# Moving the early channels' final-norm weights from VectorE to GpSimd in the last stage of a hybrid decoder layer

## The chip, the cores and the metric

One core of a Trainium2 chip runs the whole layer in one launch. The metric is the device time of an execution in microseconds (us), as the median of several runs. TensorE does the matmuls, VectorE and ScalarE the elementwise work, GpSimd small things and some DMA issues, SyncE issues most DMAs. In the profile they are PE (matmul), PEld (weight load), DVE (VectorE), ACT (ScalarE), POOL (GpSimd) and SP (SyncE).

## The reference

Tokens: 1024. Channels: 1024. All float32. The layer is a norm, an input projection, a pooling mixer and a recurrent mixer, an output projection, an MLP of width 4096, a gated per-layer input, and a final norm. Only the end bears on this case:

```python
z = rms_norm(h, norm_ple_g[l])
gate = jax.nn.sigmoid(z @ w_ple_gate[l] + b_ple_gate[l])
h = h + gate * (p[l] @ w_ple_proj[l])
return rms_norm(h, norm_final_g)      # h * rsqrt(mean(h*h) + 1e-6) * norm_final_g
```

## The kernel before

Every float32 product is made of three passes over split operands (high by high, high by low, low by high). All through the kernel the channels lie on the partitions and the tokens along the row, with one exception: the last stage. There, for the late 512 tokens and the later 512 channels (the "late" channels, numbers 512 to 1023), the gate product is turned around, so that 128 tokens lie on the partitions. There are four such token tiles, 0 to 3 (`NTOK`), and for each of them a row tile `late[i]` of 128 x 1024: its first half, `quarter(i, 0)`, holds the early channels (0 to 511), which were computed with channels on partitions and have come in turned through DRAM; the second half, `quarter(i, 1)`, holds the late channels.

For a token tile, in this order:

- TensorE: 24 matmuls of 128x512 for the gate into `ps_e` (`gate_products`, L1239) and 6 for the projection of the layer's input into `ps_j` (`token_proj`, L1263; in some tiles it goes to a bank named `ps_e`). The first of the 24 is issued ahead, in the middle of the tile before (`gate_opened`). After it, VectorE adds the gate's bias to what lies in the bank (L1248), and only then may the other 23 accumulate onto it.
- ScalarE: the sigmoid (L1278). VectorE: its product with the projection (L1283), the sum into `quarter(i, 1)` (L1285), and the sum of squares of the late channels (`mean`, L1217), which starts from `early_mean[i]`, the sum of squares of the early channels plus epsilon.
- GpSimd: `inverse(i)`, the power -0.5 of the mean (L1288), 128x1.
- VectorE: `scale_late(i)` (L1292), the late channels times the inverse and the final norm's weights. ScalarE: `scale_early(i)` (L1296), the early channels times the inverse. SyncE: `leave_for(i)` (L1301), the store of both halves.

So the early channels' share of the final norm's weights has to be multiplied in at another place: `early_gain` (L1227), after ScalarE has squared them (`early_square`, L1223), since the squares are those of the channels without weights. Behind it L1228 adds epsilon to their sum.

In this stage every VectorE, ScalarE and TensorE instruction is pinned to the order in which the code issues it (`pin`). So the order of the lines in the loop over `NTOK` is the order in each engine's queue, and an instruction that waits holds up all that stand behind it on its engine. `early(0)` issues the early work of tiles 0 and 1 in iteration 1, `early(2)` that of tiles 2 and 3 at the end of iteration 1.

Of the kernel before, what the change touches and what calls it, by code (L numbers as in the profile page):

```python
# [12 lines left out]
ALU = mybir.AluOpType  # L13
# [6 lines left out]
EPS = 1e-6  # L20
# [20 lines left out]
NTOK = 4  # L41
NQUAD = 4 * P
# [21 lines left out]
def block_kernel(  # L64
# [17 lines left out]
    nc = tc.nc  # L82
# [49 lines left out]
    def bank(name):  # L132
        return pd.tile([P, HALF], F32, tag="pd", name=name)
# [27 lines left out]
    def got(ps):  # L161
        if ps.shape[-1] > HALF:
            return ps.rearrange("p (b j a) -> p b a j", b=2, a=2)
        return ps.rearrange("p (j a) -> p a j", a=2)

    def by(x, ps):
        if ps.shape[-1] > HALF:
            return x.rearrange("p (b a j) -> p b a j", b=2, a=2)
        return x.rearrange("p (a j) -> p a j", a=2)
# [7 lines left out]
    def pin(ins):  # L177
        return tc.keep_in_program_order(ins) if in_order else ins
# [324 lines left out]
    for k in range(NT):  # L503
# [3 lines left out]
        for hs in halves:  # L507
            if k == hs.start == 0:
                whi, wlo = (t[:, :HALF] for t in weight_tiles("wl0"))
                g = col("g_mix", 0)  # L510
                x, zhi, zlo = (t[:, hs] for t in (H[0], *A[0]))
# [9 lines left out]
            x, zhi, zlo = (t[:, hs] for t in (H[k], *A[k]))  # L521
# [597 lines left out]
    early_mean, means, inverses = ([ms[:, 4 * x + i : 4 * x + i + 1] for i in range(NTOK)] for x in range(3))  # L1119
    power = pool.tile([P, 1], F32, name="power")  # L1120
# [60 lines left out]
    g_row, b_row, square = row[:, :S], row[:, S : S + NQUAD], row[:, S + NQUAD :]  # L1181
# [19 lines left out]
    def quarter(i, half):  # L1201
        return late[i][:, half * NQUAD : (half + 1) * NQUAD]
# [9 lines left out]
    def mean(i, cut=slice(0, NQUAD)):  # L1212

        n = cut.stop - cut.start
        x = quarter(i, 1).rearrange("p (g x) -> p g x", g=4)[:, :, cut.start // 4 : cut.stop // 4]
        pin(
            nc.vector.tensor_tensor_reduce(  # L1217
                square[:, :n].rearrange("p (g x) -> p g x", g=4), x, x, 1.0 / D, early_mean[i], ALU.mult, ALU.add, means[i]
            )
        )  # L1220

    def early_square(i):
        pin(nc.scalar.activation(T[5][:, SECOND], quarter(i, 0), AF.Square, scale=D**-0.5, accum_out=early_mean[i]))  # L1223

    def early_gain(i):
        x = quarter(i, 0)
        pin(nc.vector.tensor_tensor(x, x, g_row[:, :NQUAD], ALU.mult))  # L1227
        pin(nc.vector.tensor_scalar_add(early_mean[i], early_mean[i], EPS))  # L1228

    def token_slice(i):  # L1230
        return slice(HALF + i * P, HALF + (i + 1) * P)
# [19 lines left out]
    def token_gate(i, pg):  # L1251
        gate_products(i, pg, range(1, 12))
        ahead = gate_opened(i + 1) if i < NTOK - 1 else None
        gate_products(i, pg, range(12, 3 * NT))
        return ahead

    def token_proj(i, pj, cut):
        ts = token_slice(i)
        for k, (hi, lo, wh, wl) in enumerate(ple):
            for n, (z, w) in enumerate(((hi, wh), (hi, wl), (lo, wh))):  # L1260
                w = w[:, NQUAD + cut.start : NQUAD + cut.stop]
                pin(
                    nc.tensor.matmul(  # L1263
                        pj, z[:, ts], turns(w), start=k == n == 0, stop=k == len(ple) - 1 and n == 2
                    )
                )
# [7 lines left out]
    def sigmoids(i, pg, cut=slice(0, NQUAD)):  # L1274
        t = T[3 + i % 2][:, FIRST]
        whole = cut.stop - cut.start == NQUAD
        got_a, by_a = (got(pg), by(t, pg)) if whole else (got(pg)[:, cut.start // 256], t[:, cut])
        pin(nc.scalar.activation(by_a, got_a, AF.Sigmoid))  # L1278

    def gated(i, pj, cut=slice(0, NQUAD)):  # L1280

        t, e = T[3 + i % 2][:, FIRST][:, cut], T[3 + i % 2][:, SECOND][:, cut]
        pin(nc.vector.tensor_tensor(by(e, pj), by(t, pj), got(pj), ALU.mult))  # L1283
        y = quarter(i, 1).rearrange("p (g o x) -> p g o x", g=4, x=32)[:, :, cut.start // P : cut.stop // P]
        pin(nc.vector.tensor_tensor(y, y, e.rearrange("p (o g x) -> p g o x", g=4, x=32), ALU.add))  # L1285

    def inverse(i):
        nc.gpsimd.tensor_tensor(inverses[i], means[i], power, ALU.pow)  # L1288

    def scale_late(i, cut=slice(0, NQUAD)):  # L1290
        y = quarter(i, 1)[:, cut]
        pin(nc.vector.scalar_tensor_tensor(y, y, inverses[i], g_row[:, NQUAD:][:, cut], ALU.mult, ALU.mult))  # L1292

    def scale_early(i, cut=slice(0, NQUAD)):
        x = quarter(i, 0)[:, cut]
        pin(nc.scalar.activation(x, x, AF.Identity, scale=inverses[i]))  # L1296

    def leave_for(i, cut=slice(0, NQUAD)):
        to = token_out[:, i].rearrange("p (h x) -> p h x", h=2)
        tc.keep_in_program_order(  # L1300
            nc.sync.dma_start(to[:, :, cut], late[i].rearrange("p (h x) -> p h x", h=2)[:, :, cut])  # L1301
        )

    def token_last(i, pg, pj):

        cuts = slice(0, 256), slice(256, NQUAD)
        for cut in cuts:
            sigmoids(i, pg, cut)
        scale_early(i - 1)
        leave_for(i - 1)  # L1310
        gated(i, pj[0], cuts[0])
        y = quarter(i, 1).rearrange("p (g x) -> p g x", g=4)[:, :, :64]
        pin(
            nc.scalar.activation(
                T[5][:, HALF : HALF + 256].rearrange("p (g x) -> p g x", g=4), y, AF.Square, scale=D**-0.5, accum_out=means[i - 1]
            )
        )
        gated(i, pj[1], cuts[1])
        pin(nc.vector.tensor_tensor(early_mean[i], early_mean[i], means[i - 1], ALU.add))
        mean(i, cuts[1])  # L1320
        inverse(i)
        scale_early(i, slice(0, 256))
        rest = quarter(i, 0)[:, 256:]
        pin(nc.vector.tensor_scalar_mul(rest, rest, inverses[i]))
        scale_late(i)
        for half in range(2):
            nc.sync.dma_start(token_out[:, i, half * NQUAD : (half + 1) * NQUAD], quarter(i, half))

    for g, hs in enumerate(GROUPS):
# [3 lines left out]
        for n, o in enumerate(ORDER[g]):  # L1333
# [14 lines left out]
            if g == 0 and 1 <= n < 5:  # L1348
                raw = wp.tile([P, S], F32, tag="raw", name=f"wg0_{n + 3}_raw")
                nc.sync.dma_start(raw, w_gate[n + 3])  # L1350
                x = slice((n - 1) * P, n * P)
# [27 lines left out]
    def early(first):  # L1379

        for x in range(first, first + 2):
            early_square(x)
            early_gain(x)

    in_order[:] = [True]
    opened = gate_opened(0)
    for i in range(NTOK):
        end = i == NTOK - 1
        pg, pj = opened
        if end:  # L1390
            token_gate(i, pg)
            pj = [x[:, :256] for x in (pj, bank("ps_j_end"))]
            for a, x in enumerate(pj):
                token_proj(i, x, slice(256 * a, 256 * a + 256))
            token_last(i, pg, pj)
            continue
        token_proj(i, pj, slice(0, NQUAD))
        opened = token_gate(i, pg)
        if i == 1:
            early(0)  # L1400
            mean(0)
            inverse(0)
        sigmoids(i, pg)
        if i > 0:
            scale_late(i - 1)
            scale_early(i - 1)
            leave_for(i - 1)
        gated(i, pj)
        if i == 0:
            continue  # L1410
        mean(i)
        inverse(i)
        if i == 1:
            early(2)
        if i == 2:
            scale_late(i)
    in_order.clear()
# [82 lines left out]
```

## Time and profile before

| what | value |
|---|---|
| median of 3 runs | 919.86 us (919.85 to 919.89) |
| the profiled execution's own time | 919.68 us |
| its span, first to last instruction | 917.9 us |
| granted TensorE clock | 0.998 |
| TensorE matmul busy, share of the span | 99% |
| VectorE busy | 76% |
| GpSimd busy | 4%, 62 instructions |
| last stage, from the first turned gate matmul | 882.6 us to 917.9 us |

The profiled execution's time is 1.78 us over its span, and it lies 0.18 us below the median of the runs. A row of the timeline reads: start in us, duration in us, engine, line, operation, tile written and tiles read, partitions x columns, how many. In square brackets stands how long the engine had been idle before it and what ended that idle time. The rows of the waits read: who waited, for whom, us in total, times, the longest.

### The profile page before, as it was taken

Reading aid. Unit: us, or ns where it says so; the run is one execution under the profiler, and the core shown is the slowest. Engines: PE = TensorE matmul, PEld = TensorE weight load, DVE = VectorE, ACT = ScalarE, POOL = GpSimd, SP = SyncE. Lnnn points to the kernel's source line nnn. Section 1 sums busy time; section 2 is a strip of 40 time slices with the busy share of each in tenths; the row PEclk is TensorE's granted clock in tenths of the full one; section 3 lists DMA queues with packets and bytes.
Section 4 is the critical chain, followed back from the end, with each engine's and each line's share of the span. In section 5 each row is a group of like instructions: output and inputs, shape, how many; then the busy total and the mean of one; then the engine's idle time right before and its main releaser. Section 6 shows DMA issues by size and latency. Waiting matters only on the chain.

```text
span 917.9 us, 11247 instructions
## 1 busy us (share of the span) xinstructions
PE 907.8 (99%) x4221; PEld 791.2 (86%) x4221; DVE 700.8 (76%) x872; ACT 466.3 (51%) x602; POOL 39.1 (4%) x62
## 2 busy tenths in 40 slices
PE   9999999999999999999999999999999999999996
PEld 7888888888888888888888888888888888888885
DVE  7999974668876567656756899899876679799665
ACT  6569892447554454445444654353343436555322
POOL 4300001000000000000000000000000000000001
PEclk9999999999999999999999999999999999999999
DMA  7211145214478667766864987466633341041363
GB/s 273 101 47 45 48 160 144 76 46 120 111 206 223 201 167 229 224 184 176 243 196 165 355 321 278 138 202 203 205 113 100 115 161 46 1 138 47 104 181 117
DMA packets 56871, 142.47 MB, mean 155 GB/s; under 512 B 4976, under 2 KB 9968, under 8 KB 56816
## 3 DMA queue, kind: packets, MB, share of 16 engines
q1 hardware_dynamic: 52992, 132.31, 43.5%
q0 software_dynamic: 2736, 8.91, 5.8%
q10 hardware_dynamic: 1088, 0.52, 0.3%
q8 instruction: 33, 0.54, 0.3%
q14 instruction: 22, 0.18, 0.1%
HBM read 106.08 MB, written 35.65 MB: 154 GB/s over the span
## 4 chain that ended last, share of the span: by engine, by line
PE 96%; DMA 1%; DVE 1%; issue 1%; SPq 0%; POOL 0%; ACT 0%; DVEq 0%; POOLq 0%; ACTq 0%
PE ps_P_d L363 32%; PE ps_b_u L363 12%; PE ps_i L363 9%; PE ps_o L363 9%; PE ps_d_u L363 8%; PE ps_a_u L363 8%; PE ps_e L363 8%; PE ps_l L363 3%; PE ps_P_u L363 3%; PE ps_l L557 1%; PE ps_j L363 1%; PE ps_g L626 1%; PE ps_l_second L363 1%; PE ps_p L363 1%; DMA turn<-late 0%
## 5 line engine op out<-in xcount | busy, mean ns | idle before, releaser
L363 PE MATMUL ps_P_d<-a,wd_P_hi 128*128 128x512 f32 x880 | 261.8, 379 | 0.0
L363 PEld LDWEIGHTS ps_P_d<-a,wd_P_hi 128*128 128x128 f32 x880 | 166.5, 189 | 23.5
L363 PE MATMUL ps_P_d<-a,wd_P_lo 128*128 128x512 f32 x440 | 166.9, 379 | 0.0
L363 PE MATMUL ps_b_u<-a,wu_P 128*128 128x512 f32 x504 | 113.6, 379 | 0.0
L363 PEld LDWEIGHTS ps_b_u<-a,wu_P 128*128 128x128 f32 x504 | 95.3, 189 | 13.4
L363 PEld LDWEIGHTS ps_P_d<-a,wd_P_lo 128*128 128x128 f32 x440 | 83.2, 189 | 11.7
L363 PE MATMUL ps_a_u<-y,wu_P 128*128 128x512 f32 x360 | 82.6, 379 | 0.0
L363 PEld LDWEIGHTS ps_a_u<-y,wu_P 128*128 128x128 f32 x360 | 68.1, 189 | 9.6
L807 DVE TENSOR_TENSOR t_h<-t_h,ps_P_d 128x512 f32<-128x512 f32 (+1 forms) x56 | 42.4, 758 | 37.0 <-PE ps_P_d L363 37.0
L186 DVE TENSOR_TENSOR a<-wd,a 128x1024 fp32r<-128x1024 f32 x56 | 67.0, 1218 | 0.9 <-ACT a L185 0.6
L363 PE MATMUL ps_i<-a,wi_hi 128*128 128x512 f32 x256 | 66.1, 381 | 0.0
L363 PE MATMUL ps_o<-y,wo_hi 128*128 128x512 f32 x256 | 65.7, 379 | 0.0
L185 ACT ACTIVATE a<-wd 128x1024 fp32r<-128x1024 f32 x56 | 57.9, 1049 | 7.0 <-PE ps_P_d L363 7.0
L363 PEld LDWEIGHTS ps_i<-a,wi_hi 128*128 128x128 f32 x256 | 48.1, 189 | 7.9 <-PE ps_g L626 0.3
L185 ACT ACTIVATE wd_P_hi<-wd 128x1024 fp32r<-128x1024 f32 x24 | 25.3, 1056 | 58.0 <-PE ps_P_d L363 57.9
L363 PEld LDWEIGHTS ps_o<-y,wo_hi 128*128 128x128 f32 x256 | 48.4, 189 | 6.8
L825 DVE SCALAR_TENSOR_TENSOR t_h<-t_h,rstd 128x2048 f32<-128x2048 f32 x16 | 36.6, 2291 | 19.3 <-ACT t_h L844 19.3
L186 DVE TENSOR_TENSOR wu_P<-wu_raw,wu_P 128x512 fp32r<-128x512 f32 x45 | 30.9, 687 | 24.1 <-ACT wu_P L185 23.9
L186 DVE TENSOR_TENSOR wu_P<-wu,wu_P 128x512 fp32r<-128x512 f32 x47 | 32.3, 687 | 21.7 <-ACT wu_P L185 21.6
L363 PE MATMUL ps_d_u<-y,wu_P 128*128 128x512 f32 x180 | 41.3, 379 | 0.0
L363 PE MATMUL ps_d_u<-a,wu_P 128*128 128x512 f32 x180 | 41.3, 379 | 0.0
L185 ACT ACTIVATE wu_P<-wu 128x512 fp32r<-128x512 f32 x47 | 29.4, 625 | 20.0 <-PE ps_b_u L363 14.0
(252 smaller groups left out, 1538.6 us busy)
## 6 DMA issues: line engine op xcount, KB each, us to landing
wd<-act SPq DMA_DIRECT2D x56, 512.0 KB, 5.4
act<-t_h SPq DMA_DIRECT2D x32, 512.0 KB, 6.1
wu<-in_w_up SPq DMA_DIRECT2D x16, 512.0 KB, 4.9
act<-wu SPq DMA_DIRECT2D x16, 512.0 KB, 6.0
wd<-in_w_down SPq DMA_DIRECT2D x16, 512.0 KB, 5.9
wu_raw<-in_w_up SPq DMA_DIRECT2D x15, 512.0 KB, 5.3
t_h<-in_xT SPq DMA_DIRECT2D x14, 512.0 KB, 4.6
wg_raw<-in_w_gate SPq DMA_DIRECT2D x10, 512.0 KB, 3.3
```

The source lines that it names most:

```text
L185: first = pin(nc.scalar.activation(hi, src, AF.Copy))
L186: lowest[:] = [pin((eng or nc.vector).tensor_tensor(lo, src, f32(hi), ALU.subtract)).ins]
L363: ins = nc.tensor.matmul(ps, w, turns(z[:, hs]), start=first and z is zhi and w is whi, stop=last and w is wlo, skip_group_check=more,)
L557: nc.tensor.matmul(ps, kblk(w, o), turns(z[:, hs]), start=k == n == 0, stop=False)
L626: nc.tensor.matmul(x, w[r, o * P : (o + 1) * P], turns(z[r, at : at + HALF]), start=n == 0, stop=n == 2)
L807: (eng or nc.vector).tensor_tensor(to, to if y is None else y, x, ALU.add)
L825: nc.vector.scalar_tensor_tensor(cc, cc, 0.0, twice(R), ALU.max, ALU.mult)
```

## The change

Two things. The product with the weights (L1227, four times, 128x512 each) goes from VectorE to GpSimd, and its place in GpSimd's queue is fixed between the powers: tile 0's ahead of the first power, tile 1's behind it, those of tiles 2 and 3 behind the second. The addition of epsilon (128x1) stays on VectorE, in the place where the product and the addition were. The power is now pinned too.

```diff
     def early_gain(i):
         x = quarter(i, 0)
-        pin(nc.vector.tensor_tensor(x, x, g_row[:, :NQUAD], ALU.mult))
-        pin(nc.vector.tensor_scalar_add(early_mean[i], early_mean[i], EPS))
+        pin(nc.gpsimd.tensor_tensor(x, x, g_row[:, :NQUAD], ALU.mult))
...
     def inverse(i):
-        nc.gpsimd.tensor_tensor(inverses[i], means[i], power, ALU.pow)
+        pin(nc.gpsimd.tensor_tensor(inverses[i], means[i], power, ALU.pow))
...
         for x in range(first, first + 2):
             early_square(x)
-            early_gain(x)
+            pin(nc.vector.tensor_scalar_add(early_mean[x], early_mean[x], EPS))
...
         if i == 1:
             early(0)
+            early_gain(0)
             mean(0)
             inverse(0)
+            early_gain(1)
         sigmoids(i, pg)
...
         if i == 1:
             early(2)
+            for x in range(2, NTOK):
+                early_gain(x)
         if i == 2:
             scale_late(i)
```

In the rows below `late_6384` to `late_6387` are the row tiles of token tiles 0 to 3, `edge` holds the means and inverses, `t_h` the weights' row and scratch, and ISA is the sum of squares (two rows: the work, and the read of its sum). Lines behind L1228 are one less in the changed kernel.

VectorE's queue before, from the sum of squares of tile 1 to the product of tile 2's sigmoid:

```order
L1217 ISA t_h,edge<-late_6385,edge 128x512
L1217 ISA edge 128x1
L1227 TENSOR_TENSOR late_6386<-late_6386,t_h 128x512
L1228 TENSOR_SCALAR edge<-edge 128x1
L1227 TENSOR_TENSOR late_6387<-late_6387,t_h 128x512
L1228 TENSOR_SCALAR edge<-edge 128x1
L1248 TENSOR_TENSOR ps_e_3_6709<-ps_e_3_6709,t_h 128x2x256
L1292 SCALAR_TENSOR_TENSOR late_6385<-late_6385,edge,t_h 128x512
L1283 TENSOR_TENSOR t_h<-t_h,ps_j_2_6655 128x512
```

The same stretch of VectorE's queue in the changed kernel:

```order
L1217 ISA t_h,edge<-late_6385,edge 128x512
L1217 ISA edge 128x1
L1382 TENSOR_SCALAR edge<-edge 128x1 x2
L1247 TENSOR_TENSOR ps_e_3_6709<-ps_e_3_6709,t_h 128x2x256
L1291 SCALAR_TENSOR_TENSOR late_6385<-late_6385,edge,t_h 128x512
L1282 TENSOR_TENSOR t_h<-t_h,ps_j_2_6655 128x512
```

The two products no longer stand ahead of the addition of tile 3's bias (L1248, now L1247). The two of tiles 0 and 1 are likewise gone from ahead of tile 0's sum of squares.

GpSimd's queue in the changed kernel, behind the last DMA that it issues (before there were only the four powers, L1288):

```order
L1227 TENSOR_TENSOR late_6384<-late_6384,t_h 128x512
L1287 TENSOR_TENSOR edge<-edge,power 128x1
L1227 TENSOR_TENSOR late_6385<-late_6385,t_h 128x512
L1287 TENSOR_TENSOR edge<-edge,power 128x1
L1227 TENSOR_TENSOR late_6386<-late_6386,t_h 128x512
L1227 TENSOR_TENSOR late_6387<-late_6387,t_h 128x512
L1287 TENSOR_TENSOR edge<-edge,power 128x1 x2
```

Each of the powers of tiles 0, 1 and 2 now stands behind a product that ends before it can begin.

## The prediction

> **What bounds the kernel now.** I read the page's busy line first, then the waits of TensorE from 880 us on, then the timeline of that stretch, engine by engine.
>
> ```profile
> PE 907.8 (99%) x4221; PEld 791.2 (86%) x4221; DVE 700.8 (76%) x872; ACT 466.3 (51%) x602; POOL 39.1 (4%) x62
> ...
> L363 PE MATMUL ps_P_d<-a,wd_P_hi 128*128 128x512 f32 x880 | 261.8, 379 | 0.0
> ```
>
> TensorE sets the pace nearly everywhere, so the change can win only what TensorE idles in the last stage, or what lies behind its last matmul. In the last stage it waits once:
>
> ```profile
> PE ps_e L1239 <- DVE ps_e L1248: 1.1, 1, 1.1
> ```
>
> and TensorE's part of the timeline shows where:
>
> ```profile
> 897.10 5.34 PE L1239 MATMUL ps_e<-a 128*128 128x512 f32 x24
> 903.51 5.23 PE L1239 MATMUL ps_e<-a 128*128 128x512 f32 x23 [1.06 <-DVE ps_e L1248]
> 908.57 0.83 PE L1263 MATMUL ps_j<-proj,proj 128*128 128x256 f32 x6
> ```
>
> The wait is for the addition of tile 3's bias. One matmul of this size shows 0.38 us (the page's 379 ns), so 24 of them in 5.34 us start every (5.34 - 0.38) / 23 = 0.216 us, and the 25th could have started at 897.10 + 24 x 0.2157 = 902.28. It started at 903.51: 1.23 us late, more than the 1.06 of idle time shown, since matmuls overlap. The 23 after the stall took 5.23, where 22 x 0.2157 + 0.38 makes 5.13: the restart costs 0.10 more. **TensorE's loss is 1.33 us**, and that is the cap on this part. VectorE shows why the bias is late:
>
> ```profile
> 896.53 0.69 DVE L1227 TENSOR_TENSOR late<-late,t_h 128x512 f32<-128x512 f32 x1 [0.81 <-ACT t_h L1223]
> 897.14 0.15 DVE L1228 TENSOR_SCALAR edge<-edge 128x1 f32<-128x1 f32 x1
> 897.20 0.74 DVE L1217 CUSTOM_DVE_ANT_0 t_h<-late,edge 128x512 f32<-128x512 f32 x1
> ...
> 898.64 0.75 DVE L1292 SCALAR_TENSOR_TENSOR late<-late,edge,t_h 128x512 f32<-128x512 f32 x1 [0.69 <-POOL edge L1288]
> 899.31 0.68 DVE L1283 TENSOR_TENSOR t_h<-t_h,ps_e 128x512 f32<-128x512 f32 x1
> 900.03 0.69 DVE L1285 TENSOR_TENSOR late<-late,t_h 128x512 f32<-128x512 f32 x1
> 900.75 0.75 DVE L1217 CUSTOM_DVE_ANT_0 t_h<-late,edge 128x512 f32<-128x512 f32 x1
> ...
> 901.43 0.69 DVE L1227 TENSOR_TENSOR late<-late,t_h 128x512 f32<-128x512 f32 x1
> 902.03 0.15 DVE L1228 TENSOR_SCALAR edge<-edge 128x1 f32<-128x1 f32 x1
> 902.10 0.68 DVE L1227 TENSOR_TENSOR late<-late,t_h 128x512 f32<-128x512 f32 x1
> 902.70 0.15 DVE L1228 TENSOR_SCALAR edge<-edge 128x1 f32<-128x1 f32 x1
> 902.76 0.69 DVE L1248 TENSOR_TENSOR ps_e<-ps_e,t_h 128x512 f32<-128x512 f32 x1
> 903.36 0.74 DVE L1292 SCALAR_TENSOR_TENSOR late<-late,edge,t_h 128x512 f32<-128x512 f32 x1
> 904.02 0.68 DVE L1283 TENSOR_TENSOR t_h<-t_h,ps_j 128x512 f32<-128x512 f32 x1
> 904.73 0.69 DVE L1285 TENSOR_TENSOR late<-late,t_h 128x512 f32<-128x512 f32 x1
> 905.46 0.75 DVE L1217 CUSTOM_DVE_ANT_0 t_h<-late,edge 128x512 f32<-128x512 f32 x1
> ...
> 906.88 0.75 DVE L1292 SCALAR_TENSOR_TENSOR late<-late,edge,t_h 128x512 f32<-128x512 f32 x1 [0.66 <-POOL edge L1288]
> 909.51 0.42 DVE L1283 TENSOR_TENSOR t_h<-t_h,ps_j 128x256 f32<-128x256 f32 x1 [1.88 <-ACT t_h L1278]
> ```
>
> From 896.53 to 903.36 VectorE is a chain whose only rest is 0.69 us for the first power, and three of the products (L1227) stand in it. TensorE resumes 903.51 - 902.76 = 0.75 us after the bias row starts, so a bias that starts by 902.28 - 0.75 = **901.53 costs TensorE nothing**.
>
> **The change, part by part.**
>
> *VectorE loses four products.* Tile 0's (894.96) fell into idle time. For tile 1, VectorE still waits for ScalarE's square, since the addition of epsilon needs its sum; but then 0.06 us later (897.14 to 897.20) comes tile 0's sum of squares, at 896.53 + 0.06 = 896.59 in place of 897.20: 0.61 us earlier. Power, scaling, product, sum and sum of squares of tile 1 move by as much, the last to 900.14. Of the pair at 901.43 and 902.10 the additions stay, at 0.07 each, and 0.60 goes for each product: 1.20 us. The bias starts at 902.76 - 0.61 - 1.20 = **900.95**, which is 0.58 us ahead of what TensorE needs. ScalarE follows: its squares of tiles 2 and 3 stand behind a scaling that waits for the same first power, so they move by the same 0.61.
>
> ```profile
> 894.74 0.19 ACT L1223 ACTIVATION_READ_ACCUMULATOR t_h<-late 128x1 f32 x1
> ...
> 900.54 0.19 ACT L1223 ACTIVATION_READ_ACCUMULATOR t_h<-late 128x1 f32 x1
> 902.48 0.60 ACT L1278 ACTIVATE t_h<-ps_e 128x512 f32<-128x512 f32 x1 [1.75 <-PE ps_e L1239]
> ```
>
> The last sum is then there at 900.73 - 0.61 = 900.12, ahead of the additions at 900.82. The edit costs nothing there.
>
> *GpSimd gets four products.* No row of it has this shape, so its price d has to be bounded. It does run small ones:
>
> ```profile
> 0.72 0.20 POOL L384 MEMSET t_h<- 128x128 f32 x1 [0.29 <-POOLq L1486]
> ...
> 3.40 0.10 POOL L478 MEMSET sp<- 128x4 f32 x1
> ...
> 16.61 1.03 POOL L480 TENSOR_TENSOR sp<-sp 128x4 f32<-128x4 f32 x1
> ...
> 24.97 1.36 POOL L481 TENSOR_SCALAR sp<-sp 128x4 f32<-128x4 f32 x1
> 26.42 0.20 POOL L480 TENSOR_TENSOR sp<-sp 128x4 f32<-128x4 f32 x1
> ...
> L386 POOL TENSOR_SCALAR_AFFINE_SELECT t_h<-t_h 128x128 f32<-128x128 f32 x7 | 2.0, 292 | 0.5
> ```
>
> Writing alone costs (0.20 - 0.10) / 124 = 0.8 ns a column; reading and writing 128 columns took 292 ns, some 0.7 ns a column over the 0.20 us of a product of 4. So one pass over 512 columns is about 0.42 us. From below: reads hidden behind the write, 0.20 + 0.42 = 0.62. From above: two reads and the write each in its turn, 0.20 + 3 x 0.42 = 1.46. The row with one read and one write costs one pass, so two reads should cost two: **d = 1.05 us**. The Trainium skill (GPSIMD Engine Reference, section 3.1) gives 4497 ns for such a sum of 2048 columns, roughly twice VectorE, and advises against elementwise work on GpSimd; scaled to 512 columns it makes an estimate of 1.1 to 1.3, and the sum below would lose 0 to 0.24 us by it; no row here shows it.
>
> Do the products delay the powers? The powers are:
>
> ```profile
> 898.04 0.57 POOL L1288 TENSOR_TENSOR edge<-edge,power 128x1 f32<-128x1 f32 x1 [422.08 <-DVE edge L1217]
> 901.59 0.94 POOL L1288 TENSOR_TENSOR edge<-edge,power 128x1 f32<-128x1 f32 x1 [2.98 <-DVE edge L1217]
> 906.30 0.55 POOL L1288 TENSOR_TENSOR edge<-edge,power 128x1 f32<-128x1 f32 x1 [3.77 <-DVE edge L1217]
> ```
>
> Tile 0's product can start when its square is read, at 894.74 + 0.19 = 894.93 and some 0.04 for the signal, so at 894.97, and ends at 896.02; its power is wanted at 898.04 - 0.61 = 897.43. Tile 1's follows that power, 898.09 to 899.14; the next power is wanted 0.84 after the sum of squares (905.46 to 906.30), at 900.98. Tiles 2 and 3 follow from about 901.6 to 903.8. Tile 2's power is wanted later: its sigmoid ends at 902.48 + 0.60 = 903.08 as before, its product starts at 903.10, and 0.71 and 0.73 on (904.02, 904.73, 905.46) its sum of squares at 904.54, the power at 905.38. All fit. The first power came after 422 us of idle time and took no longer than the third, so I price nothing for a first use.
>
> *The two engines together.* The power at 901.59 took 0.94 against 0.55 while VectorE's product of 901.43 ran until 902.12; the small product at 16.61 took 1.03 against 0.20 at 26.42. So GpSimd is held while VectorE runs an operation with two inputs in SBUF. Whether VectorE is held by a long GpSimd product, no row shows: 0 at one end, a whole d for each at the other. Take the dear end. At 898.03 tile 0's scaling wants to start, 0.03 after the power; tile 1's product comes 0.09 after it (GpSimd's own step, from 24.97 + 1.36 to 26.42), so VectorE is first, until 898.78. The product then runs to 899.83, and the sum L1285, due at 899.42, is 0.41 late. The bias starts at 901.36: still ahead of 901.53. Up to d = 1.22 TensorE loses nothing. Further on, tile 1's scaling is wanted 2.14 after that sum, at 901.97 (0.84 and 0.60 behind its sum of squares), and ends at 902.72; behind it tile 2's product would run to 903.77 and tile 3's to 904.90, the sum of tile 2 (due at 903.81) would start there, and its scaling, 2.15 later (904.73 to 906.88), end at 907.8. The tail wants VectorE at 909.51 - 1.33 = 908.18, so that is hidden too; it is used up at the same d, 1.22, and beyond it the end comes 3 us later for each us of d, one for each of three products. The Trainium skill (SBUF — State Buffer, section "Who interferes with whom") has it that the port is an exclusive lock for such a pair of instructions, held for the whole instruction by whichever came first. The trace agrees for GpSimd's side alone; by that rule the dear end holds, and TensorE still loses nothing.
>
> *The tail.* Behind TensorE's last matmul stand the same operations as before, on the same engines, in the same order; they move as one.
>
> **The sum.** TensorE -1.33, all else 0. Against the profiled execution: 919.68 - 1.33 = 918.35, and its span 917.9 - 1.33 = 916.6. The median of the runs stands 0.18 higher: **918.53 us**, 0.14% less than before. A change of up to 0.2% (1.84 us) is about what a measurement here can't tell from none, so this counts as no change.
>
> **The rivals.**
>
> *GpSimd gets in first* (27%). If the product of tile 1 holds VectorE's scaling at 898.03 rather than the other way round, the scaling starts at 898.09 + 1.05 = 899.14, 1.11 late; the bias at 902.06, TensorE at 902.81. Gain 903.51 - 902.81 = 0.70: 919.16. For it: VectorE is only 0.06 us ahead. Against: the held power at 901.59 gave way. A d over 1.22 with VectorE first ends here too: 919.25 at the upper bound of 1.46, by 3 x 0.24.
>
> *The stall goes, the end stays* (6%): 919.86. Something else would have to hold the tail, the stores say. Against it: the store of tile 2 waits for ScalarE's scaling behind the last sigmoids, and so moves along.
>
> *Slower* (5%): GpSimd's product as the bound. Place: the wait of VectorE for it, at all four. With d over 1.62 tile 0's sum of squares starts only at 894.97 + d. Then 0.84 + 0.60 to the scaling, 0.75 + d to tile 1's sum, 2.16 to its scaling, 0.75 + 2d to tile 2's sum, 0.72 + 0.84 + 0.60 + 0.67 to the tail: 902.90 + 4d, against 909.51. It decides from d = 1.65; at 2.0 it costs 1.39 us, 921.25, and at 2.11 more than 0.2%. Against: it is over the upper bound of 1.46, and needs VectorE to be held for whole instructions.
>
> *Faster by over 1.84* (5%): the cap of 1.33 speaks against it, and nothing else in the tail is touched; this is what I can't see.
>
> **How the numbers follow.** The forecast has 57%. The range: 918.35 (the full gain and as much again as the median stands off the profile) to 919.6 (GpSimd first with a d at the upper bound, by TensorE's start: 919.16 + 0.41). Above lie the last part of the second rival and the slower one, some 12%, below some 6%. Chances: faster by over 0.2% 5%, within 92%, slower 3% (the slower rival with d over 2.11).
>
> **What would show it.** Right: TensorE's wait for L1247 is gone, the bias starts between 900.9 and 901.5, no DVE row between 896 and 908 carries L1227, GpSimd shows four products of about 1.05, the projection of tile 3 starts at 907.24, and the span is 916.6. The first rival shows as a late scaling at 898 and a TensorE wait of 0.2 to 0.6. Wrong: a product above 1.6 us, powers that start late, or a tail in which VectorE comes to its first product of tile 3 after TensorE has finished its inputs.

## The result, and the profile after

| kernel | median, us | runs | ratio to before (95% interval) |
|---|---|---|---|
| before | 919.88 | 20 | |
| the change | 918.49 | 20 | 0.9983 (0.9976 to 0.9990) |

The change is faster by 0.17%, between 0.10% and 0.24%. The forecast time (918.53 us) is 0.04 us from the median, and yet two of the steps that led to it are wrong, with errors of opposite sign. And the text had called a gain of this size no change, while the interval excludes none.

TensorE's waits in the last stage, after the change:

```profile
PE ps_e L1238 <- DVE ps_e L1247: 0.5, 1, 0.5
```

and its part of the timeline (start, duration, engine, line, tile):

```profile
897.57 5.34 PE L1238 MATMUL ps_e<-a 128*128 128x512 f32 x24
903.39 5.23 PE L1238 MATMUL ps_e<-a 128*128 128x512 f32 x23 [0.48 <-DVE ps_e L1247]
908.46 0.83 PE L1262 MATMUL ps_j<-proj,proj 128*128 128x256 f32 x6
```

Tile 3 starts 903.39 - (897.57 + 24 x 0.2157 = 902.75) = 0.64 us late; before it was 1.23. So the wait is about halved and not gone. VectorE's timeline shows what keeps it:

```profile
897.20 0.15 DVE L1382 TENSOR_SCALAR edge<-edge 128x1 f32<-128x1 f32 x1 [1.53 <-ACT t_h L1223]
897.27 0.74 DVE L1217 CUSTOM_DVE_ANT_0 t_h<-late,edge 128x512 f32<-128x512 f32 x1
...
898.71 1.78 DVE L1291 SCALAR_TENSOR_TENSOR late<-late,edge,t_h 128x512 f32<-128x512 f32 x1 [0.69 <-POOL edge L1287]
900.41 0.67 DVE L1282 TENSOR_TENSOR t_h<-t_h,ps_e 128x512 f32<-128x512 f32 x1
901.12 0.69 DVE L1284 TENSOR_TENSOR late<-late,t_h 128x512 f32<-128x512 f32 x1
...
902.65 0.69 DVE L1247 TENSOR_TENSOR ps_e<-ps_e,t_h 128x512 f32<-128x512 f32 x1
903.28 1.77 DVE L1291 SCALAR_TENSOR_TENSOR late<-late,edge,t_h 128x512 f32<-128x512 f32 x1
904.96 0.67 DVE L1282 TENSOR_TENSOR t_h<-t_h,ps_j 128x512 f32<-128x512 f32 x1
905.67 1.05 DVE L1284 TENSOR_TENSOR late<-late,t_h 128x512 f32<-128x512 f32 x1
```

and GpSimd's shows the other side:

```profile
895.57 1.27 POOL L1227 TENSOR_TENSOR late<-late,t_h 128x512 f32<-128x512 f32 x1 [419.16 <-ACT t_h L1223]
898.11 0.57 POOL L1287 TENSOR_TENSOR edge<-edge,power 128x1 f32<-128x1 f32 x1 [1.26 <-DVE edge L1217]
898.66 1.28 POOL L1227 TENSOR_TENSOR late<-late,t_h 128x512 f32<-128x512 f32 x1
902.69 0.55 POOL L1287 TENSOR_TENSOR edge<-edge,power 128x1 f32<-128x1 f32 x1 [2.75 <-DVE edge L1382]
903.21 2.97 POOL L1227 TENSOR_TENSOR late<-late,t_h 128x512 f32<-128x512 f32 x2
```

A product takes 1.27 to 1.28 us. Tile 1's starts at 898.66, 0.05 us ahead of VectorE's scaling at 898.71, and the scaling takes 1.78 in place of 0.75: 1.03 us of waiting inside an instruction, which the list of waits does not show. The same happens at 903.21 and 903.28, and the sum at 905.67 loses another 0.36.

The spans differ by 917.9 - 916.7 = 1.2 us. Tile 2 starts 0.47 later (897.57 against 897.10), tile 3's late start is 0.59 shorter: that leaves 0.12. The other 1.1 us is behind the last store. SyncE's waits in the last 13 us, the row for the last stores' landing, before

```profile
SPq L1492 <- DMA out<-late: 2.7, 2, 1.7
```

and after the change:

```profile
SPq L1495 <- DMA out<-late: 1.6, 2, 1.0
```

In the kernel before, the DMA queues between 915.3 and 916 us show what else ran there (queue, kind, packets, MB, share of the 16 engines' time):

```profile
q14 instruction: 1, 0.01, 2.8%
q1 hardware_dynamic: 4, 0.00, 2.1%
```

One packet on queue 14 is no data of the kernel: the profile names its kind "instruction". In the trace it is 8192 bytes, from 915.41 to 915.71; the last packet of the last store runs from 915.71 to 915.82, and the last landing is told at 916.76, when all the others had been told by 915.68. After the change there is no such packet. Queue 14 brings 22 transfers of 8 KB within the span, and ten of them fit VectorE's instruction count. In the kernel before (all of VectorE's records counted, waits on semaphores too):

```
transfer at, us             31.0 144.0 253.7 342.7 426.9 513.7 609.1 725.1 829.9 915.4
VectorE instructions so far   63   190   321   447   577   707   829   953  1086  1215
```

They are 128 apart in the mean ((1215 - 63) / 9). VectorE has 1218 records before and 1210 after the change. That ten of 22 fit shows little by itself; the runs that change VectorE's count alone have to show whose transfer the last one is.

### The profile page after: what moved, and what is told of

It is laid out like the page before. It is cut to its first block, busy times and chain, and to the rows that moved or that the text cites. A ratio compares the mean times of both kernels' runs of the same rounds, so it can differ in the third digit from the quotient of the medians.

```text
span 916.7 us, 11250 instructions
## 1 busy us (share of the span) xinstructions
PE 908.7 (99%) x4221; PEld 791.2 (86%) x4221; DVE 701.1 (76%) x868; ACT 466.5 (51%) x602; POOL 44.7 (5%) x66
## 4 chain that ended last, share of the span: by engine, by line
PE 96%; DVE 1%; issue 1%; DMA 1%; POOL 0%; SPq 0%; ACT 0%; DVEq 0%; POOLq 0%
PE ps_P_d L363 32%; PE ps_b_u L363 12%; PE ps_i L363 9%; PE ps_o L363 9%; PE ps_d_u L363 8%; PE ps_a_u L363 8%; PE ps_e L363 8%; PE ps_l L363 3%; PE ps_P_u L363 3%; PE ps_l L557 1%; PE ps_j L363 1%; PE ps_g L626 1%; PE ps_p L363 1%; PE ps_l_second L363 1%; DMA turn<-late 0%
```

## The experiments

Two theories of the change came out of the two traces, each with its rival. "Held": the engine that starts first holds the other, and GpSimd's product was first. "Fetch": the change took VectorE's last instruction transfer out of the last stores, by its instruction count alone. The rival of the second is "chance": one execution's late landing.

### The GpSimd products left out

```diff
-        pin(nc.gpsimd.tensor_tensor(x, x, g_row[:, :NQUAD], ALU.mult))
+        pass
```

> The changed kernel with the four GpSimd products left out altogether: the early channels of the late tokens are not multiplied by the final norm's weights, so that part of the output is missing; all else and its order stand. Theory 'held': VectorE's two scalings of 1.78 us and the sum of 1.05 us in the changed kernel are long because GpSimd's product got there first and VectorE waits for it. Then both scalings fall to 0.75, the sum to 0.69, the bias of tile 3 starts 1.1 us earlier against TensorE, TensorE's wait for it (0.48 us in the changed kernel) is gone, the late start of tile 3 (0.64 us) and the slow restart (0.10) with it: about 0.7 us less than the changed kernel, 917.8 us. Rival: the scalings are long for another reason (the power's result, the row of weights); then they stay at 1.8 us and the time stays at 918.5 us.

Measured: 917.53 us, ratio 0.9976 (0.9966 to 0.9985). VectorE:

```profile
898.19 0.75 DVE L1291 SCALAR_TENSOR_TENSOR late<-late,edge,t_h 128x512 f32<-128x512 f32 x1 [0.69 <-POOL edge L1287]
...
901.11 0.69 DVE L1247 TENSOR_TENSOR ps_e<-ps_e,t_h 128x512 f32<-128x512 f32 x1
901.73 0.75 DVE L1291 SCALAR_TENSOR_TENSOR late<-late,edge,t_h 128x512 f32<-128x512 f32 x1
```

TensorE:

```profile
897.18 10.31 PE L1238 MATMUL ps_e<-a 128*128 128x512 f32 x47
```

Both scalings are back at 0.75, and the matmuls of tiles 2 and 3 run through: 47 in 10.31 us is 46 x 0.2157 + 0.38. The long scalings came from the products, and the cap of the prediction, the whole of TensorE's late start, is what the stage gives when nothing holds VectorE.

### VectorE's instruction count, with work that does nothing

Small writes of one column, where VectorE idles 2.5 us in the first iteration of the loop; 24 in the kernel before, 8 and 24 in the changed one.

```diff
         opened = token_gate(i, pg)
+        for _ in range(24 if i == 0 else 0):
+            pin(nc.vector.memset(spread[:, 70:71], 0.0))
```

> The kernel before with 24 more writes of one column on VectorE, between the bias of tile 1 and tile 0's product, where VectorE idles 2.5 us. Theory 'fetch': VectorE's instructions come in transfers of 8 KB, one for every 128; in the kernel before the last of them falls at 915.4 us among the packets of the last stores and makes the last landing 1.08 us later (916.76 against 915.68 for the one ahead of it); in the changed kernel VectorE has 8 instructions fewer and this transfer does not come. With 24 more instructions it should come some 24 instructions earlier, about 903 us, away from the last stores: SyncE's wait for the stores falls from 2.7 to about 1.6 us, and the time to 919.88 - 1.08 = 918.8 us, though work was added and TensorE's wait of 1.06 us for the bias stays. Rival 'chance': the late landing is one execution's accident; then the time stays at 919.9 us or goes up by up to 0.1.

Measured: 918.92 us, 0.9989 (0.9981 to 0.9998), where the kernel before ran 919.96 beside it. More work on VectorE made it 1.04 us faster. TensorE's wait is still there (0.9); SyncE's wait for the stores is not:

```profile
SPq L1494 <- DMA out<-late: 1.6, 2, 1.0
```

and the trace has the transfer at 902.7 us, when 1215 records of VectorE had started, as many as in the kernel before.

> The changed kernel with 8 more writes of one column on VectorE at that same place, which gives VectorE the instruction count of the kernel before. Theory 'fetch': the 8 KB transfer is back among the last stores, SyncE waits 2.7 us for them, and the time is 918.49 + 1.08 = 919.6 us, with TensorE's wait for the bias as in the changed kernel (0.48). Rival 'chance': 918.5 us and a wait of about 1.6 us.

Measured: 919.19 us, 0.9993 (0.9984 to 1.0002): most of the change's gain is gone. The transfer is back at 914.8 us, among the last packets, and

```profile
SPq L1497 <- DMA out<-late: 2.7, 2, 1.7
```

> The control to the run with 8 more writes on VectorE: the changed kernel with 24. Theory 'fetch': the 8 KB transfer comes at about 905 us, not among the last stores; SyncE waits 1.6 us for them, and the time is that of the changed kernel, 918.5 us. Rival 'the writes themselves cost': more than with 8 of them, 919.5 us or over.

Measured: 918.01 us, 0.9979 (0.9971 to 0.9988); the transfer came at 904.7 us, and

```profile
SPq L1497 <- DMA out<-late: 1.6, 2, 1.0
```

By the ratios 8 writes cost 0.9 to 1.3 us (0.9993 against the change's 0.9983 and 0.9979, the second from a run below), and three times as many cost nothing: it is the place of the transfer that counts, not the writes. The intervals of these ratios overlap, so the charge is read from SyncE's waits and the times agree with it. "Chance" falls.

### The products back on VectorE, in its idle places

Tile 0's behind its square, tile 1's behind tile 1's scaling, tiles 2 and 3 behind tile 2's scaling.

```diff
-        pin(nc.gpsimd.tensor_tensor(x, x, g_row[:, :NQUAD], ALU.mult))
+        pin(nc.vector.tensor_tensor(x, x, g_row[:, :NQUAD], ALU.mult))
...
             early_square(x)
+            if x == 0:
+                early_gain(x)
...
             early(0)
-            early_gain(0)
             mean(0)
             inverse(0)
-            early_gain(1)
...
             scale_late(i - 1)
+            if i == 2:
+                early_gain(1)
             scale_early(i - 1)
...
             early(2)
+        if i == 2:
+            scale_late(i)
             for x in range(2, NTOK):
                 early_gain(x)
-        if i == 2:
-            scale_late(i)
```

> The changed kernel with the four products back on VectorE, but at places where it idles: tile 0's behind its square, tile 1's behind tile 1's scaling, those of tiles 2 and 3 behind tile 2's scaling; GpSimd has the four powers alone, as before. By 'held' and by the prediction's sum the bias of tile 3 starts at about 901.0 on the clock of the kernel before, TensorE does not wait, and the stage is 1.33 us shorter than before. By 'fetch' VectorE is back near its old count, the 8 KB transfer comes at the end again and costs 1.08: 919.88 - 1.33 = 918.55 us, no better than the changed kernel. By 'chance' there is no such charge, and it is 0.7 us better than the changed kernel: 917.8 us.

Measured: 917.57 us, 0.9974 (0.9965 to 0.9984). TensorE runs through the gate products of tiles 2 and 3, as expected:

```profile
896.79 10.31 PE L1238 MATMUL ps_e<-a 128*128 128x512 f32 x47
```

The time missed what "fetch" was made to say. VectorE has 1215 records here, so the transfer that came behind the 1215th in the kernel before could come only behind VectorE's last one: it ran at 916.3 us, behind the end of the span (915.2). The wait for the stores was 1.6. So two more runs moved the count by 8 and by 3:

> The kernel with the four products in VectorE's idle places, and 8 more writes of one column on VectorE. Without them its last 8 KB transfer came at 916.3 us, behind the last store's landing, since VectorE reaches its 1215th instruction only with its very last one. With 8 more it comes some 8 instructions earlier, among the last stores' packets. Theory 'fetch': SyncE's wait for the stores goes from 1.6 to 2.7 us and the time from 917.57 to 918.6 us, though TensorE still never waits in the last stage. Rival 'chance': 917.6 us.

Measured: 917.50 us, 0.9974 (0.9964 to 0.9984), a miss: the transfer came at 911.4 us, ahead of the last stores' packets, not among them, and cost nothing.

> The kernel with the four products in VectorE's idle places, and 3 more writes of one column on VectorE, which gives VectorE the 1218 instructions that the kernel before and the changed kernel with 8 more writes have. With 1215 the last 8 KB transfer came at 916.3 us, behind the last landing, with 1223 at 911.4 us, ahead of the last stores' packets (which run from 912.0 to 914.2 us there); in both SyncE waited 1.6 us. Theory 'fetch': with 1218 it falls among the packets again, 2 us behind the last VectorE instructions; SyncE's wait is 2.7 us and the time 917.5 + 1.08 = 918.6 us, with TensorE never waiting in the last stage. Rival 'chance': a wait of 1.6 us and 917.5 us.

Measured: 918.62 us, 0.9986 (0.9977 to 0.9995), with TensorE running through, as in the run without them:

```profile
897.64 10.31 PE L1238 MATMUL ps_e<-a 128*128 128x512 f32 x47
```

and SyncE's waits:

```profile
SPq L1499 <- DMA out<-late: 2.7, 2, 1.7
```

Three writes of one column, 0.31 us of VectorE in its idle time, cost 1.1 us. All three kernels with 1218 records (before, the change with 8 more, this one) have the transfer at 914.6 to 915.4 us and a wait of 2.7; the others, with 1210 to 1215, 1223, 1234 and 1242, have 1.6. In each of the three the transfer runs just ahead of the last packet of the last store; other places among the packets were not tried.

### Who starts first

> The changed kernel with one more GpSimd instruction, a write of one column, between the first power and tile 1's product, so that the product starts some 0.1 us later and VectorE's scaling of tile 0 starts first. Theory 'whoever starts first holds the other': the scaling falls from 1.78 to 0.75 us, the product grows from 1.28 to about 1.9, and now the sum of tile 1 (0.69 us) waits for what is left of it, some 0.5 us; the bias of tile 3 comes about 0.5 us earlier than in the changed kernel and TensorE's late start of tile 3 falls from 0.4 to 0.6 us to under 0.15. Time about 918.0 us. Rival 'GpSimd always goes ahead of VectorE': the scaling stays at 1.7 us and the time at 918.5.

```diff
             inverse(0)
+            pin(nc.gpsimd.memset(spread[:, 70:71], 0.0))
             early_gain(1)
```

Measured: 917.99 us, 0.9982 (0.9973 to 0.9991), and it settled nothing, since the write was too short. GpSimd's product

```profile
897.92 1.27 POOL L1227 TENSOR_TENSOR late<-late,t_h 128x512 f32<-128x512 f32 x1
```

still started 0.02 us ahead of VectorE's scaling:

```profile
897.94 1.81 DVE L1291 SCALAR_TENSOR_TENSOR late<-late,edge,t_h 128x512 f32<-128x512 f32 x1 [0.69 <-POOL edge L1403]
```

So a longer one was put there (256 scratch columns):

```diff
             inverse(0)
+            pin(nc.gpsimd.memset(T[5][:, :2 * P], 0.0))
             early_gain(1)
```

> The changed kernel with a GpSimd write of 256 scratch columns (some 0.3 us) between the first power and tile 1's product. With a write of one column the product still started 0.02 us ahead of VectorE's scaling (897.92 against 897.94), which then took 1.81 us. Now the scaling starts some 0.25 us ahead of the product. Theory 'whoever starts first holds the other': the scaling takes 0.75 us, the product is held and takes about 1.27 + 0.5 us, the sum of tile 1 (else 0.69 us) waits for its rest, about 0.5 us; the bias comes 0.4 to 0.5 us earlier, and TensorE's late start of tile 3 is at most 0.2 us. Time 0.1 to 0.5 us below the changed kernel's, about 917.8. Rival 'GpSimd goes ahead whenever it comes': the scaling is interrupted, takes over 1.7 us, and the bias comes no earlier.

Measured: 917.40 us, 0.9975 (0.9964 to 0.9985). GpSimd:

```profile
897.45 0.57 POOL L1287 TENSOR_TENSOR edge<-edge,power 128x1 f32<-128x1 f32 x1 [1.04 <-DVE edge L1217]
897.99 0.30 POOL L1403 MEMSET t_h<- 128x256 f32 x1
898.26 1.69 POOL L1227 TENSOR_TENSOR late<-late,t_h 128x512 f32<-128x512 f32 x1
```

VectorE:

```profile
898.06 0.75 DVE L1291 SCALAR_TENSOR_TENSOR late<-late,edge,t_h 128x512 f32<-128x512 f32 x1 [0.69 <-POOL edge L1287]
898.73 0.68 DVE L1282 TENSOR_TENSOR t_h<-t_h,ps_e 128x512 f32<-128x512 f32 x1
899.44 1.07 DVE L1284 TENSOR_TENSOR late<-late,t_h 128x512 f32<-128x512 f32 x1
```

Now the scaling is first and takes 0.75; the product is held and takes 1.69, to 899.95; the next VectorE operation has one input in PSUM, the memory that TensorE's matmuls write, and is not held (0.68); the sum has both in SBUF, the core's working memory, as the scaling and the product have, and is held for 0.38. The write of 256 columns, which reads nothing, ran beside the scaling and did not hold it. TensorE runs through:

```profile
897.19 10.31 PE L1238 MATMUL ps_e<-a 128*128 128x512 f32 x47
```

This is the order for which the prediction worked out its dear end, and it costs TensorE nothing, as that sum said. That the price is near the sum's 0.41 us is luck: with the product's real 1.27 us, a hold for the whole instruction would have made 898.81 + 1.27 - 899.44 = 0.64. "GpSimd goes ahead whenever it comes" falls. Tile 1's scaling was left as it was in this run: tile 2's product starts ahead of it (901.90 against 901.97), and it takes 1.76.

### The change once more

> The changed kernel as it is, for a second profile and a comparison on one chip. No 8 KB transfer among the last stores, a wait of 1.6 us for them, both scalings at 1.78 us. Tile 3's start on TensorE should be late by 0.4 to 0.65 us: the profile of the changed kernel shows 0.64, the one with 8 more writes 0.42, and in the first of them tile 1's turned half had landed 0.2 us later. Time 918.5 us.

Measured: 917.76 us, 0.9979 (0.9970 to 0.9988), below what was expected. SyncE waited 1.6, the scalings took 1.77 and 1.76. Tile 3 was late by less than 0.4 to 0.65:

```profile
897.07 10.70 PE L1238 MATMUL ps_e<-a 128*128 128x512 f32 x47
907.61 0.83 PE L1262 MATMUL ps_j<-proj,proj 128*128 128x256 f32 x6
```

The projection started at 907.61, where it could have followed the 47 matmuls at 897.07 + 47 x 0.2157 = 907.21: 0.40 us lost, of which 0.10 is the slow restart. The list of waits shows nothing of it, so an empty list does not prove that TensorE ran through. Tile 1's turned half had landed earlier against tile 2's first matmul, as ScalarE's square of it shows, in the first profile of the change (first matmul at 897.57)

```profile
896.45 0.63 ACT L1223 ACTIVATE t_h<-late 128x512 f32<-128x512 f32 x1 [0.96 <-DMA late<-turn]
```

and in this one (897.07):

```profile
895.60 0.63 ACT L1223 ACTIVATE t_h<-late 128x512 f32<-128x512 f32 x1 [0.55 <-DMA late<-turn]
```

The profiles fit one line: with *a* the start of VectorE's second addition of epsilon (in the kernels whose products stand ahead of it, of tile 1's product) counted from tile 2's first matmul,

| profile | *a*, us | tile 3 late, us | late - *a* |
|---|---|---|---|
| before | -0.57 | 1.23 | 1.80 |
| before, 24 more writes | -0.72 | 1.08 | 1.80 |
| the change | -0.37 | 0.64 | 1.01 |
| the change, 8 more | -0.59 | 0.42 | 1.01 |
| the change, 24 more | -0.51 | 0.50 | 1.01 |
| the change again | -0.71 | 0.30 | 1.01 |
| the change, a GpSimd write of one column | -0.52 | 0.52 | 1.04 |

In the last row the held scaling took 1.81 us in place of 1.78. *a* differs between executions of one kernel; at the same *a* the change is worth 1.80 - 1.01 = 0.79 us to TensorE.

## Why the forecast time was met and the prediction was wrong

- **"TensorE's loss is 1.33 us."** Right as a cap: without the products, or with them in idle places, the matmuls run through. It was not won whole: 0.79 came of it. Not said: the loss hangs on when tile 1's turned half lands, which moved it by up to 0.34 us between executions of one kernel (0.30 to 0.64 in the two profiles of the change).
- **"VectorE loses four products", the bias 1.81 us earlier.** Right. Without products the bias starts 901.11 - 897.18 = 3.93 after tile 2's first matmul, before 902.76 - 897.10 = 5.66; with the 0.06 of *a* between them the difference is 1.79.
- **d = 1.05 us.** Mis-sized: 1.27 to 1.28, inside the bounds of 0.62 and 1.46. The Trainium skill (GPSIMD Engine Reference, section 3.1) gives 4497 ns for 2048 columns, which had made an estimate of 1.1 to 1.3, and the trace agrees.
- **"VectorE is first, until 898.78."** This step failed. I gave GpSimd 0.09 us from one instruction to the next, read off a pair of small ones. It starts the next before the last has ended (898.66 against 898.11 + 0.57 = 898.68), and was 0.05 ahead. What came is the first rival, "GpSimd gets in first", which had 27%. The hold cost 1.03 us; of the 1.81 about 0.79 was left, against 0.70 by that rival's sum, whose d was too small and whose hold was taken as the whole of d, two errors that offset each other. The Trainium skill (SBUF — State Buffer, section "Who interferes with whom") says that whichever instruction starts first keeps the other out. The traces now agree for both sides on who waits; but the scaling at 898.71 ends at 900.49, 0.20 us before it could have if it had begun only at the product's end (898.66 + 1.28 + 0.75 = 900.69).
- **"Behind TensorE's last matmul stand the same operations as before ... they move as one."** This step failed too, and by more. The engines' operations do move as one; what follows them doesn't. The kernel before paid 1.08 us for an instruction transfer among its last stores, and the change, by taking records off VectorE, lost that charge. It isn't in the sum, and no rival names it; the one of "faster by over 1.84" held that nothing else in the tail is touched.
- **The sum.** TensorE 0.79 for 1.33, and 1.08 for 0: 1.87 in all. The first comparison measured 0.17% (1.6 us; the medians differ by 1.39), the second 0.21% (1.9 us; 2.10). In the first pair of profiles tile 2 starts 0.47 us later after the change, which hides part of it. That the forecast came within 0.04 us of a median is luck.
- **"So this counts as no change."** This step failed as well. The 0.2% that a measurement was said not to tell from none comes from no figure ahead of it: with 20 runs a side the interval reached 0.07% each way, so that even the 0.14% of the forecast could be told from none, and the forecast should have been faster.
- **The tail had room for the late scaling of tile 2.** Right: VectorE still idled 0.47 us ahead of its first product of tile 3, where before it was 1.88.

```profile
909.40 0.42 DVE L1282 TENSOR_TENSOR t_h<-t_h,ps_j 128x256 f32<-128x256 f32 x1 [0.47 <-ACT t_h L1277]
```

- **"It is used up at the same d, 1.22."** Wrong twice. By the text's own figures the tail's limit is 1.05 + (908.18 - 907.8) / 3 = 1.18. And with tile 0's scaling first and d at 1.27 the tail lost nothing: VectorE idled 0.65 us ahead of that product (908.27). The holds measured, 1.03 and 0.38 us, are shorter than a whole d for each.
- What is left open: how the 1.08 us of the late landing come about. The last packet runs some 0.4 us behind the one ahead of it, its landing is told 0.94 after it ends, where in the changed kernel it is 0.35; the order of the packets alone doesn't give the second part. And tile 2's first matmul comes at 896.8 to 898.0 us in these profiles; why was not tried.

## What to carry to other kernels

An operation that is moved to GpSimd off a busy VectorE can still take VectorE's time, as here, where both read two operands from SBUF at once: look for it as a longer instruction, not as a wait, and arrange who starts first, or put the work into VectorE's own idle places (917.57 us) in place of another engine. A write of 256 columns on GpSimd, which let VectorE start first, did as well (917.40 us); both are 0.2 to 1.1 us below the change's two medians (918.49, 917.76), though the intervals of the ratios overlap; that TensorE runs through in them is what speaks for them. Where a change is worth a microsecond, compare the last landing and the instruction transfers of both traces before the gain is put down to the change's own mechanism, and run the kernel with a few idle instructions more.

## What the runs showed of the hardware that was not expected

- An instruction transfer of 8 KB, one for each 128 records of VectorE, costs 1.08 us when it falls just ahead of the last packet of the last stores (three kernels), and nothing when it starts 2.8 us before that packet ends (911.4 against 914.2) or behind it (916.3). The Trainium skill (Runtime: NRT & Kernel Launch, section "Instruction fetch mechanics") tells of blocks of 16 KiB and of a cost that is mostly hidden; on VectorE the runs show 8 KB, and here it was not hidden.
- GpSimd started an instruction 0.02 to 0.03 us before the one ahead of it had ended by the profile (898.66 with an end at 898.68, 898.26 with one at 897.99 + 0.30 = 898.29), and so came 0.05 us ahead of VectorE to work that one power released for both.
- A held VectorE instruction shows as one long instruction (1.78 us for 0.75) without any wait.
